# Seven block products in place of eight for some pairs of chunks in the down projections, and the MLP norm's scale on the activations

## The chip, the cores and the metric

The kernel runs on one core of one Trainium2 chip. The engines are named as the profile names them: PE (TensorE) multiplies matrices, DVE (VectorE) and ACT (ScalarE) work element by element, POOL (GpSimd) and SP (SyncE) do little here beside starting transfers. The metric is the device time of one execution in microseconds. Before the change its median over three runs is 2177.99 us (2177.91 to 2178.13).

## The reference

It is a trunk of two layers on 256 tokens of width D = 2048, in float32. Layer 0 has a gated short convolution, layer 1 a stick-breaking attention whose keys and values come from layer 0's output. Each is followed by an MLP with squared ReLU and 8192 hidden columns. The MLP and its norms are what the change touches:

```python
def rmsnorm(x, g):
    x32 = x.astype(jnp.float32)
    y = x32 * lax.rsqrt(jnp.mean(jnp.square(x32), axis=-1, keepdims=True) + NORM_EPS)
    return (y * g.astype(jnp.float32)).astype(x.dtype)

def sq_relu_mlp(u, w_up, w_down):
    return jnp.square(jax.nn.relu(u @ w_up)) @ w_down

u = rmsnorm(h, mlp_pre_g[i])
h = h + rmsnorm(sq_relu_mlp(u, w_up, w_down), mlp_post_g[i])
```

## The kernel before

**Products in three parts.** Each float32 operand is split into a high part, rounded to the format that PE multiplies, and a low part, what is left. A product is high times high, high times low and low times high, three matmuls summed in one PSUM bank.

**The weight stream.** All weights come in chunks of 128 x 1024 float32 (512 KB) through one stream in a fixed order. `load_one` (line 125) starts a chunk's transfer on SP into one of four raw buffers (`RAW`). `high_parts` (143) has ACT write the high part (line 149), `low_part` (158) has DVE write the low part (line 160, or 162 where a gain is multiplied in), both into rings of seven tiles (`RING`). The raw buffer is free when the low part is written, and the next transfer starts then. `chunk(i)` (187) is called ahead of the matmuls of chunk i and splits on to chunk i + 4.

**The MLP.** It goes by four quarters of 2048 hidden columns. In a quarter, `up` (788) makes sixteen tiles of 128 hidden columns by 256 tokens, over 32 chunks; `hidden` (778) adds a tile's two halves from PSUM (ACT line 780, DVE 782), applies max(s, 0) * s (783) and splits the result (ACT 205, DVE 206) for the next product. Then the down projection has two groups, one for each 1024 output columns. A `Group` (240) walks over 16 chunks, each with 128 rows of the weights; a chunk has, for two blocks of 128 tokens (b) and two halves of 512 columns (c), three matmuls each, so twelve (lines 258 to 260). The group's four sums lie in four of the eight PSUM banks and are evicted at its end: in the first quarter by an ACT copy (854), later by a DVE add onto the sum so far (857). After the last quarter `post` takes them into the norm that follows.

**The norm ahead of the MLP.** What enters the MLP is h times the norm's gain, without the norm's scale 1/rms of each token. Since the squared ReLU is homogeneous of degree two, the kernel multiplies the end result by 1/rms squared instead: `squares` (458) has ACT square and sum h (463), DVE makes the reciprocal (470, 471), and the last eviction's norm takes it as `scale` (lines 366, 478, 567).

**Order.** PE runs in the order in which the program is written. DVE and ACT are ordered by a planner, except between `begin` (451) and `over` (420) of a norm, where their order is the written one too. In those stretches, the transitions, the residual sums, the transposes that feed the next product (`enter`, 442) and the splits of the next weights stand in a hand-made order; `at(delay, fn)` (225) places a step by a clock that counts matmul time in the program, with delays from `TURNS`, `ROUNDS` and `SQUARES`. In the first quarter of an MLP, the first six tiles of `up` are run together for this transition (`LEAD_UP`, lines 831 to 840), so six tiles end within one microsecond of each other.

Of the kernel before, what the change touches and what calls it, by code (L numbers as in the profile page):

```python
# [9 lines left out]
F32 = mybir.dt.float32  # L10
# [39 lines left out]

# [15 lines left out]
def trunk(ctx, tc, x, xT, vecs, rows, ws, out):  # L66
# [54 lines left out]
    last_load = [None]  # L121
    count = {"loaded": 0, "split": 0, "limit": 1 << 30, "apart": False}
    lows = []

    def load_one():
        i = count["loaded"]
# [39 lines left out]
    def low_parts(until=None):  # L166

        while lows and (until is None or lows[0] <= until):
# [5 lines left out]
            if until is None:  # L174
                break

    def split_one():
        i = count["split"]
        high_parts(i)
# [60 lines left out]
    class Group:  # L240
# [21 lines left out]
        def unit(self, b, i):  # L262
# [4 lines left out]
                    self.evict(b, c, self.ps.pop((b, c)))  # L267
            spent(UNIT)

        def last_units(self, b, edge):  # L270

            for c in range(2):
                for i in range(self.n - edge, self.n):
                    self.half(b, c, i)
                    if i == self.n - 1:
                        self.evict(b, c, self.ps.pop((b, c)))
                    spent(UNIT / 2)

    def run(groups, enter=False, leave=None):

        units = [(gr, i) for gr in groups for i in range(gr.n)]
        first, last = EDGE if enter else 0, len(units) - (leave.edge if leave else 0)
        for b in range(NB):
            for gr, i in units[:first]:
                gr.unit(b, i)
        for gr, i in units[first:last]:
            if i == 0 and gr.start is not None:
                gr.start()
            for b in range(NB):
                gr.unit(b, i)  # L290
# [27 lines left out]
    class Norms:  # L318
# [42 lines left out]
        def gained(self, b, c, src, to, scale):  # L361
# [43 lines left out]
        def round(self, i):  # L405

            if i == 0:
                low_parts()
            for b in range(NB):
                self.residual(b, 2 + i)  # L410
                self.input(b, 2 + i)
            if i == 0:
                low_parts()
                low_parts()
                allow(1)
            else:
                count["limit"] = 1 << 30
                low_parts(1 << 30)

        def over(self):  # L420
            low_parts(1 << 30)
            count["apart"] = False
            self.order.__exit__(None, None, None)
            for b in range(NB):
                at(SQUARES, lambda b=b: self.squares(b))

        def residual(self, b, c):

# [13 lines left out]
        def enter(self, b, c):  # L442
            if self.x4[c] is None:
                self.x4[c] = operand("u4")
            with tc.high_priority():
                self.entered = operand_from(self.u.pop((b, c)), self.x4[c], b, tbank())
            if c == 2:
                allow(1)
                low_parts()

        def begin(self):

# [4 lines left out]

        def squares(self, b):

            s = small("hs", 4)  # L460
            with tc.issue_after(self.entered.ins):
                for c in range(4):
                    nc.scalar.activation(self.dump()[:], piece(h[b], c), AF.Square, accum_out=s[:, c : c + 1])
            nc.vector.tensor_tensor(s[:, 0:2], s[:, 0:2], s[:, 2:4], op=ALU.add)
            nc.vector.tensor_tensor(s[:, 0:1], s[:, 0:1], s[:, 1:2], op=ALU.add)
            if self.gpre is None:
                self.hs[b] = inverse_root(s[:, 0:1], eps[:])
            else:
                r = self.hs[b] = small("rstd2")
                nc.vector.tensor_scalar(r[:], s[:, 0:1], 1.0 / D, EPS, op0=ALU.mult, op1=ALU.add)  # L470
                nc.vector.reciprocal(r[:], r[:])

    class KeyNorms(Norms):


        def square(self, b, c, src, to, scale):
            with tc.high_priority():
                nc.scalar.activation(self.dump()[:], src, AF.Square, scale=scale, accum_out=self.ss[b][:, c : c + 1])

        def root(self, b):  # L480
            with tc.high_priority():
# [4 lines left out]
        def post(self, b, c, *what):  # L486
            what = (b, c, *what)
            if (b, c) == (1, 2):
                at(KV_FIRST, lambda: self.between(what))
                return  # L490
            self.square(*what)
            if c < 3:
                self.gained(*what)
                if c == 2:
                    self.add_up(b)
            elif b == 0:
                self.root(0)
                self.due = [what]
            else:
                self.gained(*self.due.pop())  # L500
                self.add_up(1)
                self.root(1)
                low_parts()
                self.due.append(what)
                at(KV_TURNS[1][0], self.second)
                for i in range(1, 4):
                    at(KV_TURNS[0][i - 1], lambda i=i: self.turn(0, i))
                    at(KV_TURNS[1][i], lambda i=i: self.turn(1, i))
                at(KV_LATE[0], self.over)
                at(KV_LATE[1], lambda: self.rest(3))  # L510
                for i in range(NB):
                    at(KV_LATE[2], lambda i=i: self.squares(i))

        def between(self, what):

            self.enter(0, 0)
            self.square(*what)
            self.residual(0, 1)
            self.input(0, 1)
            allow(1)  # L520
# [35 lines left out]
    class OutNorms(Norms):  # L556
# [8 lines left out]
        def post(self, b, c, src, to, scale):  # L565
            t = self.pool.tile([P, 512], F32, tag="hg", name="mgg", bufs=4)[:] if c > 1 else to
            nc.scalar.activation(
                self.dump()[:], src, AF.Square, scale=scale, accum_out=self.ss[b][:, c : c + 1]
            )
            self.gained(b, c, src, t, scale)  # L570
            if (b, c) == (1, 2):
# [184 lines left out]
        y = convolution(tmp)  # L756


    def project(w, xs, n_groups, evict, shift=0):
        groups = []  # L760
        for j in range(n_groups):
            banks = [[(4 * j + 2 * b + c + shift) % 8 for c in range(2)] for b in range(NB)]
# [11 lines left out]
    def mlp(pool, i, before, after):  # L774
        u = before.x4
        part = [[None] * 4 for _ in range(NB)]

        def hidden(xs, n, ps):
            half = pool.tile([P, T], F32, tag="half", name="half", bufs=2)
            nc.scalar.activation(half[:], ps[:, T:], AF.Copy)  # L780
            s = pool.tile([P, T], F32, tag="s", name="s", bufs=3)
            nc.vector.tensor_tensor(s[:], ps[:, :T], half[:], op=ALU.add)
# [5 lines left out]
        def up(q, xs):  # L788
# [5 lines left out]
            def high(k, n, b=None, begin=True, end=False):  # L794
# [8 lines left out]
                else:  # L803
                    nc.tensor.matmul(ps[:, :, b, :], weight(0, k, n), x[:, :, b, :], start=k == 0 and b == 0, stop=False)  # L804
                if end and k == KD - 1:
                    hidden(xs, n, pss.pop(n))
                spent(TILE_HIGH if b is None else TILE_LOW)

            def low(k, n, begin=False, end=True):
# [5 lines left out]
                    skip_group_check=begin,  # L815
                )
                if end and k == KD - 1:
                    hidden(xs, n, pss.pop(n))
                spent(TILE_LOW)

            def weight(part, k, n):
# [27 lines left out]

        def add(q):  # L850
            def evict(b, c, ps):
                if q == 0:
                    part[b][c] = result()
                    nc.scalar.activation(part[b][c], ps[:], AF.Copy)
                    return
                with tc.high_priority():
                    nc.vector.tensor_tensor(part[b][c], part[b][c], ps[:], op=ALU.add)
                if q == QUARTERS - 1:
                    after.post(b, c, part[b][c], part[b][c], before.hs[b][:])
            return evict  # L860

        for q in range(QUARTERS):
            xs = [None] * 4
            up(q, xs)
            if q == QUARTERS - 1:
                turned["banks"] = [2, 3]
            run(project(W["dn", i, q], xs, 2, add(q), 2), leave=after if q == QUARTERS - 1 else None)
# [262 lines left out]
```

## Time and profile before

| | |
|---|---|
| median of three runs | 2177.99 us |
| the profiled execution's own time | 2177.66 us |
| its span | 2175.9 us |
| busy: PE, DVE, ACT | 2165.6, 1341.7, 1128.3 us |
| weights moved | 408.65 MB in chunks of 512 KB |

Busy times are the union of an engine's instructions; matmuls overlap in their pipeline, so a matmul's own duration says less than the distance from one start to the next. "x1024" is a count of instructions, "128x512 fp32r<-128x512 f32" the shapes and types of output and input. The chain of waits follows the work back from the last instruction to what released it. In the kernel's middle the stages take turns: an `up` stage of some 89 us, a down projection of some 87 us, eight of each.

### The profile page before, as it was taken

What the parts mean: (1) busy time and instruction counts of PE and PEld (TensorE: products, weight loads), DVE (VectorE), ACT (ScalarE), POOL (GpSimd) and SP (SyncE); (2) the same over time, 40 slices, a digit from 0 to 9 for tenths busy, and PEclk for the clock granted to TensorE, in tenths of its full rate; (3) what the DMA queues carried; (4) which work ended last, traced back from release to release, by engine and by line L of the source; (5) the groups of instructions that cost most, each with busy time, mean ns of one, the idle gap of its engine ahead of it and who ended that gap; (6) DMA issues with size and microseconds to landing.
All of it is one profiled execution on the core that took longest, in us unless ns stands there. A gap on an engine that the chain in (4) does not pass through costs nothing.

```text
span 2175.9 us, 28843 instructions
## 1 busy us (share of the span) xinstructions
PE 2165.6 (100%) x11074; PEld 1854.0 (85%) x11074; DVE 1341.7 (62%) x1835; ACT 1128.3 (52%) x1530; POOL 4.4 (0%) x13
## 2 busy tenths in 40 slices
PE   9999999999999999999999999999999999999998
PEld 8888888888888888888888888889888888888886
DVE  8766656854654664565666777558545645655655
ACT  7544444644543453454467888446445434544543
POOL 0000000000000000000000000000000000000000
PEclk9999999999999999999999999999999999999999
DMA  8666575666566666656575546656666666666663
GB/s 304 211 193 193 187 231 165 219 196 193 184 195 193 193 188 195 192 187 185 154 227 163 155 155 208 191 163 220 195 194 186 193 195 192 192 191 193 188 194 116
DMA packets 114762, 417.18 MB, mean 192 GB/s; under 512 B 12864, under 2 KB 13120, under 8 KB 113600
## 3 DMA queue, kind: packets, MB, share of 16 engines
q1 hardware_dynamic: 113472, 408.65, 60.5%
q0 software_dynamic: 864, 6.29, 0.8%
q8 instruction: 87, 1.43, 0.3%
q14 instruction: 51, 0.42, 0.1%
q10 hardware_dynamic: 288, 0.39, 0.1%
HBM read 413.19 MB, written 2.10 MB: 191 GB/s over the span
## 4 chain that ended last, share of the span: by engine, by line
PE 98%; ACT 1%; DMA 0%; DVE 0%; issue 0%; SPq 0%; DVEq 0%; ACTq 0%
PE up L800 20%; PE acc L258 17%; PE acc L260 17%; PE acc L259 17%; PE up L813 11%; PE acc L662 11%; PE lead L662 2%; PE up L804 1%; PE tr L211 1%; PE z L909 0%; PE o L957 0%; ACT whi L149 0%; DMA raw<-w_in 0%; DMA raw<-w_v 0%; ACT L902 0%
## 5 line engine op out<-in xcount | busy, mean ns | idle before, releaser
L160 DVE TENSOR_TENSOR wlo<-raw,whi 128x1024 fp32r<-128x1024 f32 (+1 forms) x678 | 815.7, 1214 | 654.4 <-ACT whi L149 537.8
L149 ACT ACTIVATE whi<-raw 128x1024 fp32r<-128x1024 f32 (+1 forms) x678 | 711.5, 1051 | 642.6 <-PE acc L260 452.9
L800 PE MATMUL up<-u,whi 128*128 128x512 f32 x1952 | 458.3, 390 | 0.0
L800 PEld LDWEIGHTS up<-u,whi 128*128 128x128 f32 x1952 | 361.6, 188 | 71.8
L258 PE MATMUL acc<-whi,hid 128*128 128x512 f32 x1024 | 398.4, 389 | 0.0
L260 PE MATMUL acc<-whi,hid 128*128 128x512 f32 x1024 | 398.4, 389 | 0.0
L259 PE MATMUL acc<-wlo,hid 128*128 128x512 f32 x1024 | 398.3, 389 | 0.0
L813 PEld LDWEIGHTS up<-u,wlo 128*128 128x128 f32 x2048 | 256.0, 191 | 5.8
L813 PE MATMUL up<-u,wlo 128*128 128x256 f32 x2048 | 259.0, 283 | 0.0
L259 PEld LDWEIGHTS acc<-wlo,hid 128*128 128x128 f32 x1024 | 192.2, 188 | 40.0
L260 PEld LDWEIGHTS acc<-whi,hid 128*128 128x128 f32 x1024 | 192.2, 188 | 40.0
L258 PEld LDWEIGHTS acc<-whi,hid 128*128 128x128 f32 x1024 | 192.2, 188 | 39.8
L162 DVE SCALAR_TENSOR_TENSOR wlo<-raw,gv,whi 128x512 fp32r<-128x512 f32 (+1 forms) x160 | 132.1, 854 | 43.7 <-ACT whi L149 43.1
L662 PE MATMUL acc<-u,whi 128*128 128x512 f32 x672 | 156.5, 390 | 0.0
L258 PE MATMUL acc<-whi,u 128*128 128x512 f32 x384 | 153.1, 399 | 0.1
L260 PE MATMUL acc<-whi,u 128*128 128x512 f32 x384 | 149.9, 390 | 0.0
L259 PE MATMUL acc<-wlo,u 128*128 128x512 f32 x384 | 149.7, 390 | 0.0
L149 ACT ACTIVATE whi<-raw,gv 128x512 fp32r<-128x512 f32 (+1 forms) x160 | 121.8, 801 | 51.6 <-PE acc L260 38.9
L662 PEld LDWEIGHTS acc<-u,whi 128*128 128x128 f32 x672 | 124.7, 188 | 25.0
L205 ACT ACTIVATE hid<-s 128x256 fp32r<-128x256 f32 x128 | 52.9, 418 | 106.9 <-DVE s L783 106.4
L780 ACT ACTIVATE half<-up 128x256 f32<-128x256 f32 x128 | 48.3, 382 | 93.2 <-PE up L813 49.2
L260 PEld LDWEIGHTS acc<-whi,u 128*128 128x128 f32 x384 | 72.1, 188 | 15.5
(144 smaller groups left out, 1681.5 us busy)
## 6 DMA issues: line engine op xcount, KB each, us to landing
raw<-w_up SPq DMA_DIRECT2D x256, 512.0 KB, 3.9
raw<-w_dn SPq DMA_DIRECT2D x256, 512.0 KB, 4.0
raw<-w_in SPq DMA_DIRECT2D x94, 512.0 KB, 4.0
raw<-w_out SPq DMA_DIRECT2D x32, 512.0 KB, 4.4
raw<-w_v SPq DMA_DIRECT2D x32, 512.0 KB, 4.4
raw<-w_k SPq DMA_DIRECT2D x32, 512.0 KB, 4.2
raw<-w_q SPq DMA_DIRECT2D x32, 512.0 KB, 4.1
raw<-w_wo SPq DMA_DIRECT2D x32, 512.0 KB, 3.6
```

Source lines behind the costliest of these rows:

```text
L149: rounded = nc.scalar.activation(hi[:, at], raw[i][:, at], AF.Copy, scale=1.0 if gain is None else gain)
L160: nc.vector.tensor_tensor(lo[:, at], t[:, at], hi[:, at].bitcast(F32), op=ALU.subtract)
L162: nc.vector.scalar_tensor_tensor(lo[:, at], t[:, at], gain, hi[:, at].bitcast(F32), op0=ALU.mult, op1=ALU.subtract)
L205: nc.scalar.activation(hi, src, AF.Copy)
L211: nc.tensor.transpose(to[:, j * P : (j + 1) * P], src[:, j * P : (j + 1) * P], ident[:])
L258: nc.tensor.matmul(ps[:], xh, hi[:, a], start=i == 0 and k == 0, stop=False)
L259: nc.tensor.matmul(ps[:], xh, lo[:, a], start=False, stop=False)
L260: nc.tensor.matmul(ps[:], xl, hi[:, a], start=False, stop=i == self.n - 1 and k == self.ks - 1)
L662: nc.tensor.matmul(ps[:, :cols], w, xs[:, :cols], start=k == 0 and part == parts[0], stop=k == KD - 1 and part == parts[1], skip_group_che ...
L780: nc.scalar.activation(half[:], ps[:, T:], AF.Copy)
L800: nc.tensor.matmul(ps, weight(0, k, n), x, start=begin and k == 0, stop=end and k == KD - 1, skip_group_check=end)
L813: nc.tensor.matmul(pss[n][:, :T], weight(1, k, n), x, start=begin and k == 0, stop=end and k == KD - 1, skip_group_check=begin,)
```

## The change

In each group of a down projection, two pairs of neighbouring chunks, (2, 3) and (8, 9), are multiplied as a 2 x 2 by 2 x 2 block product with seven block products instead of eight, after Strassen and Winograd. Each of the seven is still three matmuls. For this

- `split_seven` forms four sums of weight blocks on DVE and splits seven blocks of 512 columns where eight were two plain chunks; the pair takes four tiles of each ring,
- `hidden` and `sums_of` form four sums of activation blocks for a pair once per quarter, when the pair's second tile is ready, and split them,
- four of the seven products go to four further PSUM banks, that are held from chunk 2 to chunk 9, and `combine` adds them into the group's results in SBUF after chunk 9. In the first quarter it also makes these results, and the evictions at the group's end are then DVE adds in every quarter.

Beside it the norm's scale is now multiplied onto the activations ahead of the squared ReLU: `spread` makes a row of the 256 scales in all partitions (a diagonal matrix and a product with ones) and `hidden` has one more DVE multiply per tile. The squares of h are moved: six of the eight of a norm into the transition, the last two right after it. The norm behind the MLP has no scale to multiply any more.

```diff
-SQUARES = 10.0
+SQUARES = 0.5
+SPREAD = 11.5
+PAIRS = (2, 8)
...
+    def split_seven(i):
+        while count["loaded"] <= i + 1:
+            load_one()
+        a, b = raw.pop(i), raw.pop(i + 1)
+        sums = sevens[i].tile([P, 4, HALF], F32, tag="gpre", name="sums", bufs=1)
+        t1, t2, t3, t4 = (sums[:, j, :] for j in range(4))
+        b11, b12, b21, b22 = a[:, :HALF], a[:, HALF:], b[:, :HALF], b[:, HALF:]
+        for t, x, y in ((t1, b12, b11), (t3, b22, b12), (t2, b22, t1), (t4, b21, t2)):
+            nc.vector.tensor_tensor(t, x, y, op=ALU.subtract)
+        factors = []
+        for name, src in (("a", b11), ("b", b[:]), ("t", sums[:, 0:2, :]), ("u", sums[:, 2:4, :])):
...
+            nc.scalar.activation(hi[:, at], src, AF.Copy)
+            low_part(hi, lo, src, at, None)
...
+        load_one()
+        load_one()
...
+    class Mixed(Group):
...
+        def seven(self, i):
...
+            for ps, (xh, xl), (hi, lo), own in (
+                (p1, x(0, 0), b11, True), (self.ps[0, 0], x(1, 0), b21, False), (self.ps[0, 1], sums(3), b22, False),
+                (p5, sums(0), t1, True), (p6, sums(1), t2, True), (p7, sums(2), t3, True),
+                (self.ps[1, 0], x(1, 1), t4, False),
+            ):
+                nc.tensor.matmul(ps[:], xh, hi, start=own and i == PAIRS[0], stop=False)
+                nc.tensor.matmul(ps[:], xh, lo, start=False, stop=False)
+                nc.tensor.matmul(ps[:], xl, hi, start=False, stop=own and i == PAIRS[-1])
+            if i == PAIRS[-1]:
+                self.combine(*self.more)
...
             if i == 0:
                 low_parts()
                 low_parts()
+                for b in range(NB):
+                    self.hs[b] = small("hs", 4)
+                    self.square(b, 0)
+                    self.square(b, 1)
                 allow(1)
...
+            at(SPREAD, self.spread)
+
+        def spread(self):
+            ps = tbank()
+            with tc.high_priority():
+                for b in range(NB):
+                    d = self.pool.tile([P, P], F32, tag="half", name="diag", bufs=2)
+                    nc.vector.tensor_scalar(d[:], ident[:], self.hs[b][:], None, op0=ALU.mult)
+                    nc.tensor.matmul(ps[:, b * P : (b + 1) * P], ones[:], d[:], start=True, stop=True)
+                nc.scalar.activation(self.spread_to, ps[:, :T], AF.Copy)
...
             if c == 2:
+                self.square(b, 2)
                 allow(1)
                 low_parts()
...
-        def hidden(xs, n, ps):
+        def hidden(xs, n, ps, sums):
...
+            nc.vector.tensor_tensor(s[:], s[:], scale[:], op=ALU.mult)
             nc.vector.scalar_tensor_tensor(s[:], s[:], 0.0, s[:], op0=ALU.max, op1=ALU.mult)
...
+        def sums_of(x, y):
+            t = after.dump()
...
+            for to, u, v, op in (
+                (s1, a21, a22, ALU.add), (s2, s1, a11, ALU.subtract),
+                (s3, a11, a21, ALU.subtract), (s4, a12, s2, ALU.subtract),
+            ):
+                nc.vector.tensor_tensor(to, u, v, op=op)
...
+            nc.scalar.activation(hi[:], t[:], AF.Copy)
+            nc.vector.tensor_tensor(lo[:], t[:], hi[:].bitcast(F32), op=ALU.subtract)
...
-                if q == 0:
-                    part[b][c] = result()
-                    nc.scalar.activation(part[b][c], ps[:], AF.Copy)
-                    return
                 with tc.high_priority():
                     nc.vector.tensor_tensor(part[b][c], part[b][c], ps[:], op=ALU.add)
                 if q == QUARTERS - 1:
-                    after.post(b, c, part[b][c], part[b][c], before.hs[b][:])
+                    after.post(b, c, part[b][c], part[b][c])
...
+            def combine(p1, p5, p6, p7):
...
+                nc.scalar.activation(t, p1[:], AF.Copy)
+                nc.vector.tensor_tensor(u2, t, p6[:], op=ALU.add)
+                nc.vector.tensor_tensor(u3, u2, p7[:], op=ALU.add)
+                nc.vector.tensor_tensor(u4, u2, p5[:], op=ALU.add)
+                if new:
+                    nc.vector.tensor_tensor(c22, u3, p5[:], op=ALU.add)
+                    return
+                nc.vector.tensor_tensor(u2, u3, p5[:], op=ALU.add)
+                for r, v in ((c11, t), (c12, u4), (c21, u3), (c22, u2)):
+                    nc.vector.tensor_tensor(r, r, v, op=ALU.add)
```

More of the change, by code (lines that the diff above doesn't have):

```diff
@@ L277, in last_units, with __init__, both, x @@
                     spent(UNIT / 2)
+    class Mixed(Group):
+        def __init__(self, first, xs, banks, evict, sums, extra, combine, pool):
+            super().__init__(first, KD, xs, banks, evict)
+            self.sums, self.extra, self.combine = sums, extra, combine
+            self.more = None
+            for i in PAIRS:
+                sevens[first + i] = pool
+        def both(self, i):
+            if i in PAIRS:
+                self.seven(i)
+            elif i - 1 not in PAIRS:
+                super().both(i)
+        def seven(self, i):
+            b11, b21, b22, t1, t2, t3, t4 = chunk(self.first + i)
+            if self.more is None:
+                self.more = [bank(n, "more") for n in self.extra]
+            sh, sl = self.sums[i]
+            def x(k, b):
+                return [part_of(self.xs, i + k, b, j) for j in range(2)]
+            def sums(j):
+                return [t[:, j * P : (j + 1) * P] for t in (sh, sl)]
+            p1, p5, p6, p7 = self.more
+            for ps, (xh, xl), (hi, lo), own in (
[8 more added lines that the diff above has]
+                self.combine(*self.more)
+            spent(UNIT * 7 / 4)
+            spent(UNIT * 7 / 4)
     def run(groups, enter=False, leave=None):
@@ L288, in run @@
                 gr.start()
-            for b in range(NB):
-                gr.unit(b, i)
+            gr.both(i)
         if leave:
@@ L359, in add_up, with gained @@
                 nc.vector.tensor_scalar(t[:], t[:], 1.0 / D, EPS, op0=ALU.mult, op1=ALU.add)
-        def gained(self, b, c, src, to, scale):
+        def gained(self, b, c, src, to, scale=None):
             with tc.high_priority():
@@ L490, in post @@
                 return
-            self.square(*what)
+            self.result_square(*what)
             if c < 3:
@@ L516, in between @@
             self.enter(0, 0)
-            self.square(*what)
+            self.result_square(*what)
             self.residual(0, 1)
@@ L776, in mlp @@
         part = [[None] * 4 for _ in range(NB)]
-        def hidden(xs, n, ps):
+        held = {}
+        scale = pool.tile([P, T], F32, tag="scale", name="scale", bufs=1)
+        before.spread_to = scale[:]
+        def hidden(xs, n, ps, sums):
             half = pool.tile([P, T], F32, tag="half", name="half", bufs=2)
```

89 lines of the change are left out of this document (67 added, 22 removed).

## Prediction

> **What bounds the kernel now.** I read the page's top first, then PE's own waits, then windows over one `up` stage and one down projection, then the time line of PE inside a down projection.
>
> ```profile
> span 2175.9 us, 28843 instructions
> PE 2165.6 (100%) x11074; PEld 1854.0 (85%) x11074; DVE 1341.7 (62%) x1835; ACT 1128.3 (52%) x1530; POOL 4.4 (0%) x13
> PEclk9999999999999999999999999999999999999999
> PE 98%; ACT 1%; DMA 0%; DVE 0%; issue 0%; SPq 0%; DVEq 0%; ACTq 0%
> PE warm L652 <- DVE ones L83: 1.1, 1, 1.1
> PE tr L211 <- DVE h L430: 0.3, 1, 0.3
> PE lead L662 <- ACT whi L149: 0.2, 1, 0.2
> 541.30:630.20 88.90, 88.90 (x514) 78.73 (x513) 55.44 (x77) 45.68 (x63) 0.00 (x0) 1.00 0.61 190
> 630.20:717.30 87.10, 87.10 (x386) 72.13 (x385) 44.06 (x42) 34.64 (x34) 0.00 (x0) 1.00 0.64 193
> 469.76 0.39 PE L258 MATMUL acc<-whi,hid 128*128 128x512 f32 x1
> ...
> 479.96 0.39 PE L258 MATMUL acc<-whi,hid 128*128 128x512 f32 x1
> ```
>
> The chain is PE to 98%, and PE waited three times in the whole run, 1.6 us together. The windows' columns are the stretch, then busy time of PE, weight loads, DVE, ACT, POOL, the granted clock and DMA. In a down projection DVE has 44.06 of 87.1 us to do, in an `up` stage 55.44 of 88.9. The last two rows bound 46 starts of matmuls without a gap: 10.20 us by 45 steps, 0.2267 us a matmul. That step, and not the 0.39 us of one, is what a matmul costs.
>
> So every matmul taken away shortens the run by its step, as long as nobody else becomes late.
>
> **What goes.** Seven products instead of eight are 21 matmuls instead of 24 per pair. Two pairs, two groups, four quarters, two layers are 32 pairs: 96 matmuls, 96 x 0.2267 = **21.76 us**. A group shrinks from 192 x 0.2267 = 43.53 to 42.17 us. The new operands have the shapes of the old ones, so I give the 21 the same step.
>
> [...]
>
> **What PE gets.** `spread` adds, per layer, two float32 matmuls of 128 columns. The nearest row of the form is L910; sixteen such matmuls of the program are 32 records, so two records each.
>
> ```profile
> L910 PE MATMUL z<-qT,kT 128*128 128x128 f32 x32 | 6.1, 274 | 0.0
> 358.81 0.44 PE tr L211 x4
> L948 DVE TENSOR_TENSOR lb<-lb,ey 128x128 f32<-128x128 f32 x32 | 9.0, 280 | 0.0
> ```
>
> From below, four transposes of 128 columns took 0.44 us in the chain, 0.11 a record: 4 x 2 x 0.11 = 0.9 us. From above, unpipelined, 4 x 2 x 0.274 = 2.2. I take 0.9, since PE pipelines everything around it.
>
> **What DVE and ACT get.** Prices by shape, from the groups of instructions:
>
> ```profile
> L160 DVE TENSOR_TENSOR wlo<-raw,whi 128x1024 fp32r<-128x1024 f32 x670 | 812.8, 1224 | 653.4 <-ACT whi L149 536.9 <-issue 96.8 <-PE acc L662 12.7
> L149 ACT ACTIVATE whi<-raw 128x1024 fp32r<-128x1024 f32 x670 | 708.6, 1059 | 641.5 <-PE acc L260 452.9 <-PE up L800 102.8 <-PE acc L662 34.7
> L440 DVE TENSOR_TENSOR hg<-h,gpre 128x512 f32<-128x512 f32 x16 | 11.0, 689 | 0.4
> L857 DVE TENSOR_TENSOR mg<-mg,acc 128x512 f32<-128x512 f32 x48 | 31.3, 683 | 19.1 <-PE acc L260 19.0
> L782 DVE TENSOR_TENSOR s<-up,half 128x256 f32<-128x256 f32 x128 | 53.3, 420 | 0.0
> L854 ACT ACTIVATE mg<-acc 128x512 f32<-128x512 f32 x16 | 9.0, 590 | 0.4
> L463 ACT ACTIVATE sq<-h 128x512 f32<-128x512 f32 x24 | 15.0, 625 | 0.4
> ```
>
> A pair on DVE: four differences of 512 columns, 4 x 0.689 = 2.76; lows of 512 + 3 x 1024 columns, 0.69 + 3 x 1.224 = 4.36; 7.12 us where two chunks took 2.45, so +4.67. On ACT: 0.62 + 3 x 1.059 where 2.12 stood, +1.68. `combine`, once a group: one ACT copy, 0.59, and on DVE four adds from PSUM and four in SBUF, 4 x 0.683 + 4 x 0.689 = 5.49 (2.73 in the first quarter). A down projection's DVE then has 44.06 + 4 x 4.67 + 2 x 5.49 = 73.7 us in 87.04 - 2.72 = 84.3 of PE: 87%, some 5.3 us to spare per group. In the first quarter the evictions move from ACT (L854) to DVE (L857), which stays below that sum because its `combine` is shorter. ACT comes to about 43 us.
>
> In an `up` stage DVE gets sixteen multiplies by the scale, 6.7 us, and two `sums_of`, each 4 x 0.28 + 0.69 = 1.8: 55.4 + 6.7 + 3.6 = 65.8 of 88.9 us. All of this costs nothing as long as the splits stay ahead of PE. How far ahead are they?
>
> ```profile
> ACT whi L149 <- PE acc L260: 48.5, 30, 1.7
> 470.69 1.06 ACT L149 ACTIVATE whi<-raw 128x1024 fp32r<-128x1024 f32 x1 [1.66 <-PE acc L260]
> 471.78 1.22 DVE L160 TENSOR_TENSOR wlo<-raw,whi 128x1024 fp32r<-128x1024 f32 x1 [1.49 <-ACT whi L149]
> ```
>
> In the down projection of 454.3 to 541.3 ACT waited 30 times for PE to free a ring tile: the ring is full. The split that ends at 473.0 is of the chunk that takes the tile freed at 470.6; PE reaches it six chunks of 2.72 us later, at 486.9, so 13.9 us of cover. A pair takes four of the seven tiles, so while PE works on a pair at most three chunks are ready behind it: 8.2 us. The largest block of other DVE work, `combine`, is 5.5, which leaves 2.7. A pair itself takes DVE 7.1 us against PE's 4.76, a debt of 2.4 that the next plain chunks (2.72 on PE, 1.22 on DVE) repay in two.
>
> **The moved squares and the new wait.** Six of a norm's eight squares, 0.625 us and a read of the accumulator (0.19) each, go into the transition on ACT, ahead of its weight splits there. Before, they stood behind the last entry, from 386.73 on.
>
> ```profile
> 372.55 1.06 ACT L149 ACTIVATE whi<-raw 128x1024 fp32r<-128x1024 f32 x1 [3.04 <-DMA raw<-w_up]
> 376.55 0.60 ACT L217 ACTIVATE u<-tr 128x512 fp32r<-128x512 f32 x1 [2.94 <-PE tr L211]
> 386.73 0.62 ACT L463 ACTIVATE sq<-h 128x512 f32<-128x512 f32 x1
> 396.91 0.15 DVE L471 RECIPROCAL rstd<-rstd 128x1 f32<-128x1 f32 x1
> 397.98 0.71 PE up L813 x6
> 398.69 3.43 PE up L800 x15
> ```
>
> ACT idles 3.04 us ahead of 372.55, where four squares (3.3 us) now stand; the two after the third entry delay the fourth entry at 378 by 0.8 us, whose operand PE first needs at 381. I cost it at nothing; if that cover were gone it is the 0.8 us, twice. `spread` comes 11.5 us of program clock after `over`, about 1.7 us ahead of the end of the six tiles at 398.7, so near 397. Its matmuls wait on PE for the diagonal, and behind them stand the last of the six tiles and everything else on PE. In the profile the statistic was done at 397.1 without hurry; now only two squares are left when `over` comes, so I take no wait, with 0.8 us per layer as the upper end. A late scale would hold `hidden` and the low parts behind it on DVE, not PE at once: the banks of the six tiles are asked for again from the ninth tile on. In layer 1 the seventh tile takes the bank of `spread`, up to 0.5 us.
>
> **At the end** the last square loses its scale (0.625 us as in L463 instead of 0.722 as in L567), -0.1 us in the last chain.
>
> ```profile
> L567 ACT ACTIVATE sq<-mg,rstd 128x512 f32<-128x512 f32 x8 | 5.8, 722 | 16.4 <-DVE mg L857 16.3
> ```
>
> **The sum.** The profiled execution took 2177.66 us by itself (span 2175.9 and 1.7 around it). 2177.66 - 21.76 + 0.9 - 0.1 = 2156.7. The runs' median is 0.3 above that execution: **2157.0 us**. Without the small costs it would be 2156.2, so nothing much below 2155.5 is to be had.
>
> **Rivals.**
>
> *DVE late after `combine`* (partial gain). The planner fixes DVE's order. If it puts `combine` ahead of a low part that PE needs next, and `combine` itself waits for PE and the copy, the block is 5.5 + 0.6 + one chunk of idle, 2.72: 8.8 us against 8.2 of cover, 0.6 us a group, 9.9 us in sixteen: 2167. For it: 87% load. Against: lows of 1.224 us start every 1.16 us where they stand in a row, so the load is overstated, and each `up` stage refills the ring.
>
> ```profile
> 387.47 4.62 DVE L160 TENSOR_TENSOR wlo<-raw,whi 128x1024 fp32r<-128x1024 f32 x4
> ```
>
> *The raw buffers* (slower). A pair holds two of the four raw buffers for DVE's whole 7.1 us, and only then start the transfers of two later chunks.
>
> ```profile
> GB/s 304 211 193 193 187 231 165 219 196 193 184 195 193 193 188 195 192 187 185 154 227 163 155 155 208 191 163 220 195 194 186 193 195 192 192 191 193 188 194 116
> DMA to landing us min/median/max: 3.3/4.0/10.4
> L133 SPq DMA_DIRECT2D raw<-w_up x256: 327/328/468, 336.0 to 2053.2; - x128
> ```
>
> DVE has the two other raw chunks meanwhile, 2.45 us, and idles L - 2.45 after each pair if a chunk lands L after the release. At the median of 4.0 that is 3.1 us of the 5.3 spare per group: no loss. If the second of two transfers lands only after both are issued (2 x 0.33) and moved at the highest rate seen (524 KB at 304 GB/s, 1.72), L = 6.4: 2 x 3.95 - 5.3 = 2.6 us a group, 42 us in sixteen, about 2198. Below L = 5.1 it costs nothing, at 5.8 it eats the gain, above 5.9 the run is slower than before. Against: a median of 4.0 over the whole run, and the 13.9 us of cover with which a quarter's down projection starts, which pays for part of it.
>
> *Nothing gained*: L between 5.7 and 5.9 above, or PE slowed by the products' new order of banks so that 21 take as long as 24: 2177 to 2178. Each matmul still loads its own weights and writes one bank as before, so little speaks for it.
>
> *The rate is not the step*: a removed matmul is worth less than 0.2267 us because the stream waits elsewhere in the same rhythm. [...] The 46 even starts speak against it. [...]
>
> **Chances.** Forecast 0.70, `combine` late 0.13, rate 0.03, nothing gained 0.06, raw buffers 0.08. Within 0.2% (4.4 us, about what a measurement of this kernel can tell from no change) is 2173.6 to 2182.3. Faster 0.86, same 0.06, slower 0.08. The range 2155.5 to 2167.5 takes in the forecast with its unknown costs and the two partial cases; it leaves out the last two cases and some tails, about 0.18.
>
> **What would show it.** Right: PE records 11074 - 96 + 8 = 10986, starts inside a pair 0.227 us apart, PE's waits still a few us in all, DVE near 74 us busy in a down window of 84.3, ACT waiting for PE to free ring tiles less often. Wrong: PE or its weight loads waiting for wlo inside pairs or just behind chunk 9 (`combine`); DVE's differences waiting for raw (the buffers); PE waiting at `spread` near the end of the six tiles.

## The result, and the profile after

| | before | after |
|---|---|---|
| median (lowest to highest), us | 2177.95 (2177.91 to 2178.13) | 2160.84 (2159.99 to 2161.86) |
| profiled execution, its span, us | 2177.66, 2175.9 | 2160.03, 2158.3 |

The changed kernel takes 0.9921 of the time before, 95% interval 0.9904 to 0.9939: 17.1 us less, where 21.0 were forecast. The top of the page of the changed kernel, with its clock, and below it PE's own waits:

```profile
span 2158.3 us, 29349 instructions
PE 2146.0 (99%) x10986; PEld 1837.0 (85%) x10986; DVE 1610.2 (75%) x2363; ACT 1177.6 (55%) x1616; POOL 4.4 (0%) x13
PEclk9999999999999999999999999999999999999999
```

```profile
PE acc L290 <- DVE wlo L163: 2.3, 1, 2.3
PE warm L755 <- DVE ones L85: 1.1, 1, 1.1
PE acc L289 <- ACT tk L1133: 0.3, 1, 0.3
```

PE has 88 records fewer, 10986 as forecast, and bounds the run still. DVE has 268 us more work and ACT 49, and neither shows in PE's waits but once: one wait of 2.3 us for a low part. It is new. (Much of DVE's new work is in the splits: two plain chunks are four blocks of 512 columns, and a pair splits seven in their place. The eight of the block product are products, not blocks.)

To find where the time went I took each stage's length on PE, from its first matmul to that of the next stage (for the last down projection, to its last matmul), and compared the two traces. The table is worked out from all matmuls of the two traces:

| stage | before, us | after, us | difference |
|---|---|---|---|
| each of seven down projections | 87.04 (87.53 for the one that ends layer 0) | 84.32 (84.78) | -2.72 to -2.75 |
| the last down projection | 86.81 | 86.67 | -0.14 |
| `up`, first quarter, layers 0 and 1 | 92.60 | 93.18, 93.15 | +0.58, +0.55 |
| the six other `up` stages | 88.90 | 88.91 | 0.0 |
| all that is ahead of layer 0's MLP | | | +0.17 |
| the attention | | | +0.37 |
| what follows the last down projection | 8.70 | 8.61 | -0.09 |

It adds up to -17.6 us, the difference of the spans. A down projection has lost 12 matmuls of 0.2267 us, 2.72 us, to the hundredth, in seven cases of eight. The eighth gained as much and lost 2.58 us again. The windows over three of them, the last among them, and over one `up` stage (columns: the stretch, busy time of PE, weight loads, DVE, ACT, POOL, granted clock, DMA share and GB/s):

```profile
454.44:538.76 84.32, 84.32 (x374) 69.82 (x373) 62.95 (x70) 41.97 (x44) 0.00 (x0) 1.00 0.64 203
538.76:627.67 88.91, 88.91 (x514) 78.75 (x513) 67.46 (x110) 45.15 (x64) 0.00 (x0) 1.00 0.59 186
...
800.89:885.21 84.32, 84.32 (x374) 69.82 (x373) 67.31 (x78) 41.98 (x44) 0.00 (x0) 1.00 0.63 201
2062.40:2146.50 84.10, 81.82 (x361) 67.45 (x360) 68.57 (x87) 40.15 (x52) 0.00 (x0) 1.00 0.48 154
```

PE is busy for the whole of the first three windows. In the fourth, the last down projection, it is idle for 2.28 us. The time lines of DVE and then of PE at that place show why:

```profile
2128.76 0.69 DVE L1004 TENSOR_TENSOR mg<-mg,more 128x512 f32<-128x512 f32 x1
2129.37 1.22 DVE L163 TENSOR_TENSOR wlo<-raw,whi 128x1024 fp32r<-128x1024 f32 x1
...
2132.23 0.69 DVE L997 TENSOR_TENSOR more<-more 128x512 f32<-128x512 f32 x1
2132.83 0.68 DVE L998 TENSOR_TENSOR more<-more 128x512 f32<-128x512 f32 x1
2133.43 0.69 DVE L1004 TENSOR_TENSOR mg<-mg,more 128x512 f32<-128x512 f32 x1
2134.03 0.69 DVE L1002 TENSOR_TENSOR more<-more 128x512 f32<-128x512 f32 x1
2134.63 1.29 DVE L1004 TENSOR_TENSOR mg<-mg,more 128x512 f32<-128x512 f32 x2
2135.83 1.23 DVE L163 TENSOR_TENSOR wlo<-raw,whi 128x1024 fp32r<-128x1024 f32 x1
```

```profile
2134.44 0.39 PE L289 MATMUL acc<-whi,hid 128*128 128x512 f32 x1
2137.11 0.50 PE L290 MATMUL acc<-wlo,hid 128*128 128x512 f32 x1 [2.28 <-DVE wlo L163]
```

Lines 996 to 1004 are `combine`. Six of its adds, from 2132.23 to 2135.83, stand ahead of the low part of the very last chunk, which ends at 2137.06; PE was ready for it at 2134.67. Elsewhere PE reaches that chunk a chunk's time (2.72 us) after the one before. Here it doesn't: `last_units` goes through chunks 10 to 15 for one output block first, then for the next. So the last of six low parts is due 16 matmuls, 3.6 us, after the pair (8, 9) has ended. Since the pair holds four of seven ring tiles, the last chunks can only be split when it gives them back, and by then the written program has issued `combine`. At the end of layer 0's MLP the same walk covers the last four chunks only (`EDGE` is 4, `OUT_EDGE` 6); there the last low part is due 34 matmuls, 7.7 us, after the pair, and PE did not wait for one.

The four runs differ by their mean granted clock: two took 2160.0 us at 0.999, two 2161.6 and 2161.9 at 0.998. The last section comes back to that.

### The profile page after: what moved, and what is told of

The parts are those of the page before. It is cut to its first block, busy times and chain, and to the rows that moved or that the text cites. A ratio compares the mean times of both kernels' runs of the same rounds, so it can differ in the third digit from the quotient of the medians.

```text
span 2158.3 us, 29349 instructions
## 1 busy us (share of the span) xinstructions
PE 2146.0 (99%) x10986; PEld 1837.0 (85%) x10986; DVE 1610.2 (75%) x2363; ACT 1177.6 (55%) x1616; POOL 4.4 (0%) x13
## 4 chain that ended last, share of the span: by engine, by line
PE 97%; ACT 1%; DVE 1%; DMA 1%; issue 0%; SPq 0%; DVEq 0%; ACTq 0%
PE up L926 21%; PE acc L291 14%; PE acc L289 14%; PE acc L290 14%; PE up L939 11%; PE acc L765 11%; PE more L357 1%; PE more L356 1%; PE more L358 1%; PE lead L765 1%; PE up L930 1%; PE acc L357 1%; PE acc L356 1%; PE acc L358 1%; PE tr L242 1%
## 5 line engine op out<-in xcount | busy, mean ns | idle before, releaser
L163 DVE TENSOR_TENSOR wlo<-raw,whi 128x1024 fp32r<-128x1024 f32 (+1 forms) x614 | 734.9, 1212 | 335.4 <-ACT whi L152 262.4
L152 ACT ACTIVATE whi<-raw 128x1024 fp32r<-128x1024 f32 (+1 forms) x614 | 637.6, 1048 | 420.9 <-PE acc L291 230.2
L290 PE MATMUL acc<-wlo,hid 128*128 128x512 f32 x768 | 298.9, 389 | 2.3 <-DVE wlo L163 2.3
L289 PE MATMUL acc<-whi,hid 128*128 128x512 f32 x768 | 298.8, 389 | 0.0
L291 PE MATMUL acc<-whi,hid 128*128 128x512 f32 x768 | 298.8, 389 | 0.0
L290 PEld LDWEIGHTS acc<-wlo,hid 128*128 128x128 f32 x768 | 144.1, 188 | 32.6 <-DVE wlo L163 2.7
L289 PEld LDWEIGHTS acc<-whi,hid 128*128 128x128 f32 x768 | 144.2, 188 | 29.9
L291 PEld LDWEIGHTS acc<-whi,hid 128*128 128x128 f32 x768 | 144.1, 188 | 29.9
```

The costliest lines, as they stand in the source:

```text
L152: rounded = nc.scalar.activation(hi[:, at], raw[i][:, at], AF.Copy, scale=1.0 if gain is None else gain)
L163: nc.vector.tensor_tensor(lo[:, at], t[:, at], hi[:, at].bitcast(F32), op=ALU.subtract)
L289: nc.tensor.matmul(ps[:], xh, hi[:, a], start=i == 0 and k == 0, stop=False)
L290: nc.tensor.matmul(ps[:], xh, lo[:, a], start=False, stop=False)
L291: nc.tensor.matmul(ps[:], xl, hi[:, a], start=False, stop=i == self.n - 1 and k == self.ks - 1)
```

## The experiments

Theory A, from the trace: the products taken away are worth their step and everything beside them is hidden, but for `spread` (1.1 us) and one late low part at the end (2.6 us). The rivals are those of the prediction: a removed product is worth less than its step; DVE is generally at its limit behind `combine`; the raw buffers are.

**The last splits ahead of `combine`** (e1). In `seven`:

```diff
             if i == PAIRS[-1]:
+                while len(stream) - count["split"] <= 3 and count["split"] < len(stream):
+                    split_one()
                 self.combine(*self.more)
```

> The last three chunks of the stream are split ahead of the last combine in the program, nothing else is changed. Theory A (the 3.8 us that the changed kernel falls short of the forecast are one wait of PE at its end, 2.6 us, for a low part that stands behind combine in DVE's fixed order, and spread's 1.1 us instead of 0.9): the wait goes, the median falls by 2.3 to 2.6 us, to about 2158, and the last down projection is 2.7 us shorter than before like the seven others. Theory B (DVE's higher load delays PE a little in many places): the time stays within 0.5 us of 2160.8.

Measured: 2157.24 us (2156.89 to 2157.58), 0.9905 of before, interval 0.9889 to 0.9922. PE's waits:

```profile
PE warm L757 <- DVE ones L85: 1.1, 1, 1.1
PE acc L289 <- ACT tk L1135: 0.2, 1, 0.2
```

The wait for the low part is gone, and the last down projection is 84.09 us long, 2.72 less than before. That one late low part was all that the down projections fell short of. Between the medians the edit brings 3.6 us, more than the 2.58 of this stage. The profiled executions differ by 3.1 us, 0.6 of it in the stretches ahead of layer 0's MLP and in the attention, whose code is the same; the rest of the 3.6 lies in the spread of the changed kernel's four runs. The theory of many small delays, with a time within 0.5 us of 2160.8, falls.

**The norm's scale alone** (e2): no pairs, and the first quarter's evictions again by ACT.

```diff
-PAIRS = (2, 8)
+PAIRS = ()
...
             def evict(b, c, ps):
+                if q == 0:
+                    part[b][c] = result()
+                    nc.scalar.activation(part[b][c], ps[:], AF.Copy)
+                    return
```

> No pairs: all chunks go by eight products, only the norm's scale on the activations, the moved squares and spread remain of the change. Theory A: two spreads of 0.56 us each and nothing else, 2178.9 to 2179.3 us, and no wait of PE at the end. Theory B: the extra DVE multiplies and the earlier squares cost more than that, 2180 us or above.

Measured: 2179.29 us (2178.49 to 2180.34), 1.0006 of before, interval 0.9997 to 1.0015. The trace has +0.59 and +0.58 us in the two `up` stages with `spread` and nothing in any down projection. The interval takes in no change at all, so the runs alone do not show a cost; by the trace the new norm costs 1.17 us on PE, and it gains nothing.

**The pairs alone** (e3): the old norm with its scale at the end. The core of the edit:

```diff
-            at(SPREAD, self.spread)
...
-            nc.vector.tensor_tensor(s[:], s[:], scale[:], op=ALU.mult)
...
-                    after.post(b, c, part[b][c], part[b][c])
+                    after.post(b, c, part[b][c], part[b][c], before.hs[b][:])
```

> Seven products for the two pairs, but the norm as it was before (scale squared at the end, no spread, no multiply in hidden, squares behind the transition). Theory A: the changed kernel's time less 1.1 us, about 2159.7, with the wait at the end still there. Theory B: DVE has 54 us less to do, so PE is delayed less, 2157 or below.

Measured: 2160.48 us (2159.62 to 2160.61), 0.9919 of before, interval 0.9904 to 0.9933. The first quarters' `up` stages are back at their old length (+0.01 and 0.00), seven down projections lose 2.72 us, the last one waits 2.28 us as in the changed kernel. At the median it is only 0.4 us faster than the changed kernel, though it has no `spread`: in the profiled execution the last down projection comes out 1.49 us longer than before, not 0.14 shorter, since PE's granted clock drops to 0.50 behind the wait (last section). DVE has less to do here and the wait is as long as before, so the theory that a lighter DVE would delay PE less (2157 us or below) falls. The pairs carry the whole gain, and the late low part at the end comes with them, not with the new norm.

**One pair instead of two**, with e1's edit (e5): `PAIRS = (2,)`.

> One pair (2, 3) per group instead of two, splits first at the end as in the run before. Theory A (a matmul is worth its step of 0.2267 us): 48 matmuls less than before the change, 2178.0 - 10.9 + 1.1 + 0.2 = 2168.4 us. [...]

Measured: 2168.96 us (2168.57 to 2169.23), 0.9958 of before, interval 0.9943 to 0.9973. Each down projection is 1.36 us shorter, 6 x 0.2267. The gain is proportional to the matmuls, at the step of 0.2267 us, and the rival, a removed matmul that is worth less, falls.

**Three pairs instead of two**, with e1's edit (e4): two more buffers for sums; three constants are moved or merged to make room for them.

```diff
-PAIRS = (2, 8)
+PAIRS = (2, 5, 8)
...
-            hi, lo = (pool.tile([P, 512], F32R, tag="hg", name="sums", bufs=4) for _ in range(2))
+            hi, lo = (pool.tile([P, 512], F32R, tag="hg", name="sums", bufs=6) for _ in range(2))
```

> Three pairs of eight in seven products (pairs 2, 5 and 8), on top of e1 (2157.24 us); three constants are moved or merged to make room in SBUF. PE still bounds: 3 products of 0.2267 us less per pair, 16 further pairs, 48 x 0.2267 = 10.88 us less, 2146.4 us, each down projection 81.6 us on PE. DVE's load would be about 67.3 + 2 x 4.3 = 76 of 81.6 us. Rival, DVE late: between two pairs stands one plain chunk alone, so the debt of 2.4 us per pair is not repaid, two pairs and the combine run 3 us or more past the cover in each of sixteen groups, 2157 + 48 - 11 = 2194 us or more, with PE waiting for low parts. Rival, raw buffers: DVE's differences wait for raw before the second and the third pair, with only one other chunk to split meanwhile; at 4 us of landing 1.5 to 3 us per pair, which shows as PE waits from 2 us a group on (2178 us).

Measured: 2146.56 us (2146.19 to 2147.24), 0.9857 of before, interval 0.9842 to 0.9871. This is the fastest kernel of the study, 14.3 us ahead of the changed one. PE's waits and the window over the second quarter's down projection:

```profile
PE warm L751 <- DVE v L806: 1.1, 1, 1.1
PE lead L761 <- ACT whi L146: 0.9, 1, 0.9
...
```

```profile
626.92:709.88 82.96, 82.96 (x367) 68.73 (x366) 75.06 (x91) 45.31 (x48) 0.00 (x0) 1.00 0.63 204
```

DVE is busy for 75.06 of 82.96 us, 90%, and PE still waits for nothing in it. The down projection is 4.08 us shorter than before, 18 x 0.2267. (The expectation's 81.6 us for it takes the third pair's gain off twice; its total of 2146.4 doesn't.) By the prediction's prices the one plain chunk between two pairs does not repay the debt that a pair leaves on DVE, and yet nobody is late.

**How much more fits on DVE** (e7): e1 with eight further adds at the end of each `combine`, whose result is not used.

```diff
+            def combine(*p):
+                parts_of(*p)
+                w = pool.tile([P, 4, 512], F32, tag="gpre", name="more", bufs=1)
+                for _ in range(8):
+                    nc.vector.tensor_tensor(w[:, 0, :], part[0][2 * j], part[0][2 * j], op=ALU.add)
```

> e1 with eight further adds of 512 columns on DVE at the end of each combine (their result is not used): 8 x 0.61 = 4.9 us a group. The prediction's arithmetic (8.2 us of cover behind a pair, 5.5 + 0.6 + 2.72 used): 13.7 against 8.2, 5.5 us a group, sixteen groups, 2245 us. Theory that the load of the whole stage counts, and not the single block, because the order on DVE puts low parts between the adds and the ring refills in time: 67.3 + 2 x 4.9 = 77.1 of 84.3 us, PE is not late, 2157 to 2159 us.

Measured: 2175.06 us (2172.99 to 2176.43), 0.9987 of before, interval 0.9977 to 0.9996, 17.8 above e1. Neither number was hit, and the trace says where both were wrong. Six of the eight down projections keep their 84.32 us, with DVE now at 75.00 of them. The loss is at two places, the ends of the two MLPs: of the 19.0 us by which its span exceeds e1's, 11.4 are in the last down projection of layer 0, 1.8 in that of layer 1 and 4.2 behind it. (Another 1.4 lie ahead of layer 0's MLP, where the code is the same.) The longest waits of PE, and the window over a down projection in the middle:

```profile
PE tr L242 <- DVE h L531: 7.5, 1, 7.5
PE acc L290 <- DVE wlo L163: 1.7, 2, 1.0
```

```profile
629.01:713.33 84.32, 84.32 (x373) 69.85 (x372) 75.00 (x92) 41.28 (x44) 0.00 (x0) 1.00 0.61 199
```

At those two ends the evictions, the norm and the transposes for what follows stand behind the adds on DVE, and PE has nothing else to do. Not all of the 11.4 us is waiting: PE stands idle for 7.45 us and 0.96 us, and behind the long idle its granted clock is at half until 1071.3 (the execution's mean is 0.997, e1's 0.999), for 4.0 us in which PE works again, an estimated 2 us more. In the middle of the kernel the cover is far longer than I had worked out. The order on DVE around a `combine` of the changed kernel, and PE's first use of one of the low parts there:

```profile
650.52 1.22 DVE L163 TENSOR_TENSOR wlo<-raw,whi 128x1024 fp32r<-128x1024 f32 x1 [1.49 <-ACT whi L152]
651.66 0.68 DVE L1004 TENSOR_TENSOR mg<-mg,more 128x512 f32<-128x512 f32 x1
652.26 1.22 DVE L163 TENSOR_TENSOR wlo<-raw,whi 128x1024 fp32r<-128x1024 f32 x1
653.40 0.68 DVE L996 TENSOR_TENSOR more<-more 128x512 f32<-128x512 f32 x1
...
667.62 1.22 DVE L163 TENSOR_TENSOR wlo242t<-sums,whi242t 128x1024 fp32r<-128x1024 f32 x1
```

```profile
677.96 0.39 PE L357 MATMUL more<-wlo242t,sums 128*128 128x512 f32 x1
```

The planner puts low parts between the adds of `combine`. The third block of the next group's first pair (chunk 242) is split at 668.8 and PE needs it at 678.0, 9.1 us later. In e7 the same rows read:

```profile
675.51 1.23 DVE L163 TENSOR_TENSOR wlo242t<-sums,whi242t 128x1024 fp32r<-128x1024 f32 x1 [0.49 <-ACT whi242t L197]
```

```profile
678.88 0.39 PE L357 MATMUL more<-wlo242t,sums 128*128 128x512 f32 x1
```

The eight adds have eaten 7 of the 9.1 us: the sums of the next pair share a buffer with `combine`'s results and wait for the last add. 2.1 us are left, and PE isn't late. So 4.9 us more a group fit in the middle; no run tried more there. In the last quarters, where PE waits for 0.3 us in each MLP for the same block of the last group's first pair, they are already a little too much.

**Three raw buffers instead of four** (e6): e1 with `RAW = 3`.

> e1 with three raw buffers instead of four. While a pair holds two, DVE has one other chunk (1.2 us) to split. Cover theory: DVE idles about 4.0 - 1.2 = 2.8 us more often for raw, 5.6 us a group against 8.5 us of idle time that DVE has per group (84.3 - 67.3 in a down projection, halved), so the waits for raw grow from 29 us to some 90 to 120 us and PE still waits for nothing: 2157 to 2160 us. Raw rival: the two transfers behind a pair land 6.4 us after the release, 2 x 5.2 = 10.4 us a group, 1.9 us past the idle time, sixteen groups, 2187 us or more, with PE waiting for wlo.

Measured: 2187.36 us (2183.93 to 2196.91), 1.005 of before, interval 1.0028 to 1.0071. That is the raw rival's number, by luck (the five runs lie 13 us apart), and not its mechanism. The profiled execution is one of the longer ones, 2192.14 us. Six of its eight down projections, with 24 pairs, last 84.32 us, as with four buffers, and DVE's waits ahead of the sums are what they were (e1, and then e6):

```profile
DVE sums L189 <- DMA raw<-w_dn: 29.3, 28, 3.1
```

```profile
DVE sums L189 <- DMA raw<-w_dn: 29.0, 33, 2.0
ACT whi L152 <- DMA raw<-w_up: 156.8, 123, 6.2
PE tr L242 <- ACT tk L1135: 7.8, 4, 2.7
PE up L932 <- DVE u L249: 6.9, 2, 3.5
```

What waits is ACT's split of the next weights at the entry of an MLP (6.2 us at once), and behind it, in the written order, the transpose's copy that PE needs. Of the 35.2 us by which the profiled span of e6 exceeds e1's, 13.0 are in the first quarters' `up` stages, 12.5 in the attention, 3.8 ahead of layer 0's MLP and 6.0 at the ends of the two MLPs. Part of it is PE's clock (0.994 in the execution's mean): at six of these places the granted clock is at half for 3.4 us, an estimated 1.4 to 1.7 us each, some 10 us together. The total agreed with a theory that the trace refutes, so it needed a control.

**Three raw buffers in the kernel before** (e8): `RAW = 3` there, no pairs.

> The kernel before with three raw buffers, as a control for e6_raw3 (2187.36 us, 30 us over e1, with no time lost in seven of the eight down projections of its trace). Theory that the lost time belongs to the transitions and the attention, where the splits are in a fixed order, and not to the pairs: the kernel before loses 20 to 30 us as well, 2198 to 2208 us, its down projections stay at 87.04 us. Rival, that pairs holding two buffers are what costs: without pairs three buffers do, 2178 to 2182 us.

Measured: 2202.3 us (2201.54 to 2204.61), 1.0115 of before, interval 1.0099 to 1.0132: 24 us lost without a single pair. Its down projections stay at 87.04 us, and the same step waits:

```profile
PE up L804 <- DVE u L218: 7.2, 2, 3.9
PE tr L211 <- ACT tk L978: 7.0, 4, 2.4
```

So the fourth buffer is needed by the transitions and the attention. With three of them the pairs themselves cost PE nothing in the middle of the kernel; only at the ends of the MLPs is there something (6 us) that the kernel before doesn't lose. (In the attention and ahead of layer 0's MLP the trace of e6 loses 5.4 us more than that of e8; its execution is 4.8 us above its median and has six drops of the clock against three.)

## Why the prediction was right, and where it was off

*The step.* 96 matmuls at 0.2267 us, 21.76 us: right, up to the wait at the end. Each down projection shows 2.72 us for 12; one pair shows 1.36 for 6 (e5), three 4.08 for 18 (e4). The case called the rate, a removed matmul worth less than its step, had a chance of 0.03 and shows in no run.

*`spread`.* 0.9 us forecast, and that is what it costs: the four records of a layer start 0.11 us apart, and with the matmul behind them PE loses 0.44 us a layer, 0.9 in all. Its wait didn't come; the copy of the scale ran without any:

```profile
396.96 0.60 PE L523 MATMUL tr<-diag,ones 128*128 128x128 f32 x4
398.74 0.36 ACT L524 ACTIVATE scale<-tr 128x256 f32<-128x256 f32 x1
```

*The moved squares.* The two `up` stages are 1.13 us longer, not 0.88. The remaining 0.25 stands 14 us ahead of `spread`, where PE reaches the transposes for the fourth piece of h 0.11 us later in each layer, in the changed kernel and in e2, and not in e3, where the squares are at their old place. The rows say where it comes from, before and then after (the stage starts 0.17 us later in the second trace):

```profile
377.99 0.59 ACT L217 ACTIVATE u<-tr 128x512 fp32r<-128x512 f32 x1
381.43 0.69 DVE L440 TENSOR_TENSOR hg<-h,gpre 128x512 f32<-128x512 f32 x1
```

```profile
378.77 0.58 ACT L248 ACTIVATE u<-tr 128x512 fp32r<-128x512 f32 x1
381.91 0.69 DVE L539 TENSOR_TENSOR hg<-h,gpre 128x512 f32<-128x512 f32 x1
```

L217 and L248 are ACT's copy of an operand as it enters, L440 and L539 DVE's product with the gain that those transposes read. A moved square ahead of it delays the copy by 0.6 us (the prediction had 0.8); in DVE's written order the product comes 0.3 us later with it, and that accounts for the 0.11 us. The prediction had followed the delay to PE's use of that operand alone and put it at nothing.

*DVE and ACT hidden.* Right in that both stay below PE's time; the size was too high for DVE: it is 62.95 to 67.31 us busy in the down projections shown (68.57 in the last), where 73.7 were forecast. Adds of 0.68 us start every 0.60 us and low parts of 1.22 every 1.14 (the rows from 650.52 on), so prices by duration are too high by a tenth; ACT came to 42 of 43 forecast, and in `up` DVE to 67.5 of 65.8. ACT waits for PE to free a ring tile less often, as foreseen: 188 times and 264 us in the splits of plain chunks, with the pairs' own splits 219 times and 298 us, where it was 321 times and 492 us:

```profile
ACT whi L152 <- PE acc L291: 263.9, 188, 1.9
```

*The cover.* This step of the prediction failed, though the time stayed within its range. The prediction had 8.2 us of cover behind a pair, with `combine` as a block of 5.5 and 2.7 left, everywhere alike. In the middle the block doesn't exist, low parts stand between its adds, and the one quoted from just behind it is 9.1 us early; e7 put 4.9 us more in at no cost there. At the end of the last group the cover is less than the prediction's: it counted 2.72 us per chunk, but `last_units` asks for the last of six chunks after 3.6 us. The rival "DVE late after `combine`" named the right mechanism, a low part behind `combine`, and priced it at 0.6 us in each of sixteen groups. It happened once, at 2.58 us, so the rival's price was wrong too. I had not looked at the written order of the last group.

*The raw buffers.* The forecast that they cost nothing held. DVE's sums wait 26 times for a transfer in the changed kernel, 28.5 us together, 1.1 each, and ACT waits 49 us for `up`'s transfers, where it was 18; the cover takes both: seven down projections lose their full 2.72 us and the later `up` stages stay as they were.

*The bank, the end.* Nothing and -0.09 us, as forecast.

*The sum.* Against the profiled execution 2156.7 were forecast and 2160.03 measured. The difference of 3.3 us is 2.58 for the late low part, 0.25 for the moved squares, and 0.54 ahead of layer 0's MLP and in the attention. Whether the last is an effect of the change is open: in e1's trace, with the same code there, the two stretches differ from before by -0.27 and +0.19, so much of it varies from one execution to the next; but the attention is 0.1 to 0.6 us longer than before in each of the seven other traces with four raw buffers. With e1's edit the wait is gone and the kernel takes 2157.24 us, 0.2 from the 2157.0 of the forecast. The median lies 0.8 above the profiled execution where I had added 0.3, since two of the four runs are longer by 1.6 us or more. Both rivals on the other side, the raw buffers past their point and PE slowed by the order of banks, didn't happen.

## What to carry to other kernels

In this kernel, where PE works without gaps, a matmul taken away was worth its step of 0.2267 us with one, two and three pairs, and the work that replaced it on other engines was free until its cover was used up; so count the cover in time up to PE's next use of the tile, and count it separately for every place where the order changes, the last group and the transitions above all. A block of work on an engine with a planned order is not a block: look what the planner puts between. And a total that agrees with a theory proves little until the trace shows the wait at the theory's place; e6 met its rival's number by luck, for another reason.

## What the runs showed of the hardware that I had not expected

The idle of 2.3 us at the end is followed, in some executions, by a drop of PE's clock. Windows of 2 us at that place in e3 and then in the changed kernel (the granted clock is the number behind POOL's 0.00 (x0)):

```profile
2134.00:2136.00 2.00, 0.19 (x1) 0.19 (x2) 1.76 (x3) 0.00 (x0) 0.00 (x0) 1.00 0.00 0
2136.00:2138.00 2.00, 2.00 (x7) 1.58 (x7) 1.38 (x3) 0.70 (x2) 0.00 (x0) 0.67 0.00 0
2138.00:2140.00 2.00, 2.00 (x7) 1.52 (x6) 0.44 (x4) 0.12 (x2) 0.00 (x0) 0.50 0.00 0
```

```profile
2136.00:2138.00 2.00, 0.89 (x4) 0.76 (x5) 1.17 (x2) 0.00 (x0) 0.00 (x0) 1.00 0.00 0
2138.00:2140.00 2.00, 2.00 (x11) 1.64 (x10) 1.65 (x5) 0.72 (x2) 0.00 (x0) 1.00 0.00 0
```

PE's time line in e3:

```profile
2135.81 0.50 PE L290 MATMUL acc<-wlo,hid 128*128 128x512 f32 x1 [2.28 <-DVE wlo L163]
...
2136.62 0.57 PE L290 MATMUL acc<-wlo,hid 128*128 128x512 f32 x1
2136.98 0.63 PE L291 MATMUL acc<-whi,hid 128*128 128x512 f32 x1
...
2139.97 0.45 PE L289 MATMUL acc<-whi,hid 128*128 128x512 f32 x1
```

In e3 the clock falls to half about 0.8 us after PE has work again, and matmuls start 0.43 us apart: eight steps take 3.35 us, from 2136.62 to 2139.97, where 1.81 would do, 1.5 us more. In the changed kernel's profile, after the same idle of 2.28 us, the clock stays at 1.00. Why one execution has the drop and the other hasn't, no run shows.

The other traces have more such places. Behind the warm-up and ahead of the last matmul, PE stands idle for more than 1.5 us fifteen times in the ten traces, all in the changed kernel, e3, e6, e7 and e8. The eight gaps of 2.38 us and longer all come with a drop of the clock to half, which starts inside the gap or up to 1.3 us behind it. Of the seven from 1.7 to 2.3 us, three do (1.98 and 2.27 us in e6, 2.28 in e3) and four don't (1.74 in e6, 1.91 and 2.24 in e8, 2.28 in the changed kernel). Each drop lasts 3.41 us, in two cases twice that. The window over the drop in e6 behind the gap of 1.98 us, in which PE is idle from 1066.61 to 1068.59:

```profile
1069.27:1072.67 3.40, 3.40 (x9) 2.64 (x9) 1.35 (x2) 2.24 (x4) 0.00 (x0) 0.50 0.02 5
```

Of the executions of the changed kernel at 2161.6 and 2161.9 us there is no trace. That they had the same drop is an inference: it would make them 1.5 us longer than the others, and they are 1.6 to 1.9 longer. In e3 three of four executions have the lower mean clock of 0.998, and they are 0.8 to 1.0 us longer than the fourth. A stall of 2.3 us on PE cost 2.3 us in one trace here, and 3.8 in the other.
